# A hybrid attention, state-space and expert block on one core: the last gate unit's split, stand-in products, and the place of the embeddings' projection

## The chip, the cores and the metric

One core of a Trainium2 chip runs the whole kernel in one launch. The metric is the device time of an execution in microseconds, and of several executions the median. Engines have these names: PE is TensorE (matmul), PEld its weight loads, DVE is VectorE, ACT is ScalarE, POOL is GpSimd, and SP is SyncE, whose queue issues nearly all loads.

## The reference, cut to what matters

One layer on 256 tokens of width 1024, all in fp32. A mixer (attention of 8 heads beside a state-space scan) adds to `x`; then a mixture of 16 experts, in which each token uses two; then a gate on token embeddings `p`; then a norm.

```python
h2 = rms_norm(x, ffn_norm_g)
x = x + hier_moe(h2, w_rg, b_rg, w_re, b_re, w_gate, w_up, w_down)  # silu(h@w_gate[e]) * (h@w_up[e]) @ w_down[e]
x = x + sigmoid(x @ w_ple_gate) * (p @ w_ple_proj)
return rms_norm(x, final_norm_g)
```

`p` is 256x256, `w_ple_proj` 256x1024 and `w_ple_gate` 1024x1024. All 16 experts' weights are read, 3 x 2 MB each.

## The kernel before, in words

**Tiles and loads.** On-chip memory is cut into 51 buffers of 128x1024 fp32 (`UNITS`, 512 KB each). Weights and intermediate results share them. One list (`pending`, lines 187 to 277) gives the order of all weight loads; `pump` (line 153) takes the next entries from it whenever buffers come free, and issues them on SP's queue at line 160, in order. A first dry pass (`Ring`) counts how many buffers each step holds, so that no load takes a buffer which a later step needs before that load is used up. A load into a buffer waits on the chip for the last reader of the buffer. `consumed` (line 164) gives a weight's buffer back.

The list holds the input projections, the output projections (`wo`, the last of the mixer), then the embeddings `pin` and the two halves `pj` of their projection (`queue_proj`, line 212), then the experts in six blocks: for each block the gate tiles `g`, the up tiles `u` and the down tiles `d`. The first four blocks hold two experts each, and the last two blocks four each. Behind the sixth block's tiles come the units `pg_0` to `pg_7` of the embeddings' gate, mixed with the last down tiles (`d_r`, the quarters `d_2` and `d_3`) and the final gain.

**Order of the work.** Every engine runs its instructions in the order in which the program emits them; the program below is that order.

1. The mixer, as a list of pieces up to `wo`. Into it hooks are set (`at`, lines 1349 to 1357); the one at `W + 3` runs `pp_T` (line 1306 on), four transposes of `pin` on PE and a copy on ACT.
2. The first chain (lines 1402 to 1420): norm, router logits, `route`, ranks and one-hot matrices. TensorE has gaps here while DVE works. `pp_fill` (line 1324) puts products of the embeddings' projection into them, one 128x256 fp32 product at a time, 16 in all: one at line 1405, five and two in `route` (1000, 1025), two in the first block's gate (1161), and three twice at line 1509. `pp_end` (line 1330) evicts the four results to two buffers, with ACT and DVE.
3. The blocks (loop at line 1475): `gate_up` (matmuls at line 1168), `hidden_T` (1187), `down` (1198) or `half_down` (1455). Before the sixth block stands `overflow`, whose body is under a branch (line 1245) that is not taken unless an expert has too many tokens.
4. The tail (lines 1610 to 1686): the sixth block's down product comes in quarters of 256 columns. Of each quarter, `q_ev` (1445) evicts with ACT (`yh`) and DVE (`yl`), `q_sum` (1527) adds it to the tokens on PE, `q_x2` (1534) adds `x` on DVE, and `q_T` (1540) transposes and splits it. Between them run the gate's products `pg` (lines 389 to 391), for which each unit is split in two parts: `wh_pg` on ACT (line 377) and `wl_pg` on DVE or POOL (line 380). At lines 1641 to 1643 the splits of units 6 and 7 are emitted, and only then the fourth quarter's products and eviction, `q_down(3)`.

Of the kernel before, what the change touches and what calls it, by code (L numbers as in the profile page):

```python
# [92 lines left out]
def emit(ctx, tc, ring, x, p, mix_norm_g, w_in, conv_w, conv_b, dt_bias,  # L93
# [75 lines left out]
    def bank(i, name):  # L169
        return psum.tile([P, 512], F32, tag=f"b{i}", name=name)  # L170
# [44 lines left out]
            pending.append((f"pj_{i}", rows(w_ple_proj, i * P * D, 1, D, D), 1))  # L215

    queue_tok("wo", w_out)
    queue_proj()

    def expert(x, src):  # L220
        if x not in regs:
# [29 lines left out]
    for bl in range(NB):  # L251
        for w, src in (("g", w_gate), ("u", w_up)):
            for c in range(4):
                for e in members(bl):
                    pending.append((f"{w}{e}_{c}", w_rows(e, src, c), 2))
        if bl < NB - 2:
            for c in range(4):
                for e in members(bl):
                    pending.append((f"d{e}_{c}", d_rows(e, c), 1))
        else:  # L260
            queue_half(bl, "h", 0)


# [733 lines left out]

    def route():
        b = MO["lg"]
        pp_fill(5)  # L1000
        for i in range(2):
            dve.scalar_tensor_tensor(rt[:, i, :], b[:, 32 * i:32 * i + 20], rs2[:, i:i + 1], rb, op0=OP.mult,
                                     op1=OP.add)


        v = rt.rearrange("p i (s e) -> p (i s) e", s=5)
        c, df = MO["cmp"]
        for d in (1, 2, 3):
            dve.tensor_tensor(c[:, :, d - 1, 3:7 - d], v[:, :, 0:4 - d], v[:, :, d:4], OP.is_ge)
        above = c if dry else bass.AP(tensor=c.tensor, offset=c.offset + 2, ap=[c.ap[0], [21, 10], [6, 3], [1, 4]])  # L1010
        dve.tensor_tensor(df[:, :, 1:4, :], above, c[:, :, :, 3:7], OP.subtract)
        dve.tensor_reduce(rk, df.rearrange("p s d e -> p s e d"), op=OP.add, axis=AX)
        rv = rk.rearrange("p (i s) e -> p i s e", i=2)
        og, re_ = rc[:, 0:8].rearrange("p (i g) -> p i g", i=2), rv[:, :, 1:5, :]
        be = lambda a: a[:, :, :, None].to_broadcast([P, 2, 4, 4])
        dve.tensor_scalar(og, rv[:, :, 0, :], 0.0, None, op0=OP.is_equal)
        dve.scalar_tensor_tensor(mskb.rearrange("p i (g e) -> p i g e", g=4), re_, 1.5, be(og), op0=OP.is_lt,
                                 op1=OP.mult)
        b = accbank("rank")
        pe.matmul(b[:, 0:16], stri, mskb[:, 0, :], start=True, stop=True)  # L1020
        pe.matmul(b[:, 16:32], stri, mskb[:, 1, :], start=True, stop=False)
        pe.matmul(b[:, 16:32], onesb, mskb[:, 0, :], start=False, stop=True)
        for i in range(2):
            pe.matmul(b[:, 32:48], onesb, mskb[:, i, :], start=(i == 0), stop=(i == 1))
        pp_fill(2)
        MO["count"] = b[:, 32:48]
        MO["rank"] = b[:, 0:32].rearrange("p (i e) -> p i e", i=2)

        def weights():

            gl, el = rt[:, :, 0:4], rt[:, :, 4:20].rearrange("p i (g e) -> p i g e", g=4)
            o1, o2, d = (o12[:, j].rearrange("p i (g e) -> p i g e", g=4) for j in range(3))
            gx = rc[:, 8:16].rearrange("p (i g) -> p i g", i=2)
            gmax, gsum, sv, w1, w2 = (rc[:, 16 + 2 * j:18 + 2 * j] for j in range(5))
            bg = lambda a: a[:, :, None].to_broadcast([P, 2, 4])
            b4 = lambda a: a[:, :, None, None].to_broadcast([P, 2, 4, 4])
            dve.tensor_reduce(gmax, gl, op=OP.max, axis=AX)
            dve.tensor_scalar(o1, re_, 0.0, None, op0=OP.is_equal)
            dve.tensor_scalar(o2, re_, 1.0, None, op0=OP.is_equal)
            dve.tensor_tensor(gx, gl, bg(gmax), OP.subtract)  # L1040
            dve.tensor_tensor(d, o1, o2, OP.subtract)
            act.activation(gx, gx, AF.Exp)
            dve.tensor_tensor(o1, o1, be(og), OP.mult)
            dve.tensor_tensor(d, d, be(og), OP.mult)
            dve.tensor_tensor(o2, o2, be(og), OP.mult)
            dve.tensor_tensor(d, d, el, OP.mult)
            dve.tensor_reduce(sv, o12[:, 2], op=OP.add, axis=AX)
            dve.tensor_reduce(gsum, gx, op=OP.add, axis=AX)
            act.activation(sv, sv, AF.Exp, scale=-1.0)
            dve.scalar_tensor_tensor(w1, sv, 1.0, gsum, op0=OP.add, op1=OP.mult)  # L1050
            dve.reciprocal(w1, w1)
            dve.tensor_tensor(w2, sv, w1, OP.mult)
            cb = comb[:, :, 0:16].rearrange("p i (g e) -> p i g e", g=4)
            dve.tensor_copy(comb[:, :, 16], rs2)
            dve.tensor_tensor(o1, o1, b4(w1), OP.mult)
            dve.tensor_tensor(o2, o2, b4(w2), OP.mult)
            dve.tensor_tensor(cb, o1, o2, OP.add)
        return weights
# [92 lines left out]
    def gate_up(pr, mo, beside=None):  # L1151
# [3 lines left out]
        for w in ("g", "u"):  # L1155
            b = accbank(f"{w}{pr}")
            for c in range(4):
                if pr == 0 and w == "g":
                    if c == 0:
                        gather_first()  # L1160
                        pp_fill(2)
                        xg = XT[0]
                    elif c < 3:
                        gather(0, c + 1, c + 2)
                for k in range(2):
                    kk = 2 * c + k
                    for s, e in enumerate(members(pr)):
                        pe.matmul(b[part(pr, s), :], xg.k(kk)[:, part(pr, s, s0)], ready[f"{w}{e}_{c}"][0][:, k, :],  # L1168
                                  start=(kk == 0), stop=(kk == KD - 1), skip_group_check=True)
                for e in members(pr):  # L1170
                    consumed(f"{w}{e}_{c}")
                if beside is not None:
                    next(beside, None)
# [68 lines left out]
    def overflow():  # L1242
# [54 lines left out]
                            pe.matmul(bx[2 * i + hf], ident, o, start=False, stop=False, skip_group_check=True)  # L1297
        ov.free()


    pp = {}

    def pp_T():
        pn = ready["pin"][0]
        pin = pn[:, 0:512].rearrange("p (i f) -> p i f", i=2)
        pp["T"] = pn[:, 512:1024].rearrange("p (k t) -> p k t", k=2)
        b = bank(4, "pT")
        for k in range(2):
            for i in range(2):
                pe.transpose(b[:, T * k + P * i:T * k + P * i + P], pin[:, i, k * P:(k + 1) * P], ident)  # L1310
        act.activation(pp["T"], b.rearrange("p (k t) -> p k t", k=2), AF.Copy)

    def pp_steps():
        for i, hf in ((1, 0), (0, 1), (1, 1), (0, 0)):
            b = bank(2 * i + hf, f"pp{i}{hf}")
            for q in range(2):
                for k in range(2):
                    c = slice(512 * hf + 256 * q, 512 * hf + 256 * q + 256)
                    pe.matmul(b[:, 256 * q:256 * q + 256], pp["T"][:, k, i * P:(i + 1) * P],
                              ready[f"pj_{k}"][0][:, 0, c], start=(k == 0), stop=(k == 1), skip_group_check=True)  # L1320
                    yield
            pp[i, hf] = b

    def pp_fill(n):
        if "g" not in pp:
            pp["g"] = pp_steps()
        for _ in range(n):
            next(pp["g"], None)

    def pp_end():  # L1330
        pp_fill(17)
        pp["t"] = Act("pp", 2).t
        for i, hf in ((1, 0), (0, 1), (1, 1), (0, 0)):
            o = pp["t"][i][:, 512 * hf:512 * hf + 512]
            if hf == 0:
                act.activation(o, pp[i, hf], AF.Copy)
            else:
                dve.tensor_copy(o, pp[i, hf])
        for k in range(2):
            consumed(f"pj_{k}")  # L1340
        consumed("pin")
# [5 lines left out]
        (early if before else hooks).setdefault(i, []).extend(fs)  # L1347

    W = P_OB
    at(W + 3, pp_T)  # L1350
    at(W + 4, lambda: x1_half(0, 0, 4, act))
    at(W + 5, lambda: x1_half(1, 0, 4, dve))
    at(W + 7, lambda: x1_scale(0), ranks_space, lambda: x1_hi(0, 0, 4), lambda: x1_lo(0, pool, 0, 4))
# [48 lines left out]
    x1_scale_end()  # L1402
    x1_half(1, 6, 8, dve)
    x1_logits_sum()
    pp_fill(1)
    x1_logits(6, 8)
    MO["x1T"].free()
    MO["S"] = Act("S", 1, F32R)
# [66 lines left out]
    for pr in range(NB):  # L1475
# [21 lines left out]
        for i in range(2):  # L1497
# [8 lines left out]
                k2 = 2 * (pr % 2) + i  # L1506
                gather(pr // 2 + 1, k2, k2 + 1)
            if pr == 0:
                pp_fill(3)
            if i == 0:  # L1510
                hidden_T(pr, mo)
        if pr == 0:
            pp_end()
        if pr == NB - 2:
            half_down(pr, mo["hT"], cw, "h", 0)
        else:
            down(pr, mo, cw)
# [88 lines left out]
    def store(i, h, q=sp):  # L1606
        s = slice(512 * h, 512 * h + 512)
        q.dma_start(dram(out, i * P * D + 512 * h, [[D, P], [1, 512]]), sc.t[i][:, s])

    half_down(NB - 1, mo["hT"], cw, "h", 0)  # L1610
    q_sum(0)
    q_sum(1)
    pg_split(0)
    q_x2(0)
    q_x2(1)
    q_T(0)
    q_T(1)
    pg_split(1)
    pg(0, 0)
    pg_split(2)  # L1620
# [18 lines left out]
    pg(4, 0)  # L1639
    pg(5, 0)  # L1640
    pg_split(6, False)
    pg_split(7, False)
    q_down(3)
    pg(4, 1, (0,))
    q_sum(3)
    q_x2(3)
# [69 lines left out]
```

## Time and profile before

| | us |
|---|---|
| median of 3 runs | 496.77 (496.36 to 500.08) |
| time of the profiled execution | 498.48 |
| its span, first to last instruction | 496.8 |
| busy in it: PE / PEld / DVE / ACT / POOL | 464.2 / 318.3 / 209.0 / 183.2 / 125.0 |

The profiled execution is one run and not the median one; 1.7 us of its time lie outside the span. A busy PE is not PE at its peak, since ends of matmuls are modelled. In a timeline, what stands in brackets behind a row is the idle time of the engine before it and what ended it. The clock is the share of 2.4 GHz that TensorE was granted: 1.00 is 2.4 GHz, 0.5 would be 1.2 GHz, and a value between is a mix of the two over a stretch.

### The profile page before, as it was taken

How to read it: one execution, taken by the hardware profiler on the slowest of the kernel's cores; microseconds unless marked ns; L12 is line 12 of the kernel's file. 1: busy time of each engine (PE TensorE's matmuls, PEld its weight loads, DVE VectorE, ACT ScalarE, POOL GpSimd, SP SyncE). 2: the span in 40 equal slices, each digit the busy share in tenths (PEclk: the TensorE clock that was granted, in tenths of full speed). 3: DMA queues.
4: the chain of work that ended last, by engine and by line, in shares of the span. 5: the costliest groups of instructions: out<-in, count | busy, mean ns of one | idle time of the engine just before them, and what ended most of it. 6: DMA issues, size and time to landing. Idle time of an engine off the chain costs nothing.

```text
span 496.8 us, 8088 instructions
## 1 busy us (share of the span) xinstructions
PE 464.2 (93%) x3001; PEld 318.3 (64%) x3001; DVE 209.0 (42%) x411; ACT 183.2 (37%) x333; POOL 125.0 (25%) x83
## 2 busy tenths in 40 slices
PE   6999999999999999999999999999999588889981
PEld 5997898999988999998754344353532121126551
DVE  5422587796569576754545111011110000023345
ACT  4646667644676364443532112020110000122233
POOL 3847634534689631042400000000000000010000
PEclk8899999999999999999999999999999899999997
DMA  8899997621423598859458999999999999999902
GB/s 286 241 338 350 350 348 234 201 86 44 127 87 122 174 390 310 271 186 373 161 194 300 393 412 409 409 408 410 409 407 392 405 408 408 396 396 372 369 34 85
DMA packets 73270, 145.25 MB, mean 292 GB/s; under 512 B 8244, under 2 KB 41352, under 8 KB 73224
## 3 DMA queue, kind: packets, MB, share of 16 engines
q1 hardware_dynamic: 72936, 143.89, 80.5%
q10 hardware_dynamic: 288, 0.79, 0.5%
q8 instruction: 25, 0.41, 0.3%
q14 instruction: 21, 0.17, 0.1%
HBM read 143.61 MB, written 1.05 MB: 291 GB/s over the span
## 4 chain that ended last, share of the span: by engine, by line
PE 54%; DMA 33%; DVE 7%; ACT 2%; issue 1%; SPq 1%; POOL 0%; DVEq 0%; ACTq 0%
DMA u<-in_w_up_dram 10%; DMA g<-in_w_gate_dram 10%; PE ac_gb L411 5%; PE ac_ob L411 5%; PE ac_ga L411 5%; DMA d_h<-in_w_down_dram 4%; DMA d<-in_w_down_dram 4%; PE ac_xs L411 3%; PE g L1168 3%; PE u L1168 3%; PE ac_q L411 3%; PE ac_bc L411 2%; PE ac_z L411 2%; PE ac_k L411 2%; DMA d_r<-in_w_down_dram 2%; PE y L1198 2%
## 5 line engine op out<-in xcount | busy, mean ns | idle before, releaser
L1168 PE MATMUL u<-u,XT 128*64 128x512 f32 (+1 forms) x256 | 55.8, 597 | 3.2 <-DMA u<-in_w_up_dram 3.1
L1168 PE MATMUL g<-g,XT 128*64 128x512 f32 (+1 forms) x256 | 50.2, 623 | 6.0 <-PEq L1245 4.6
L380 POOL TENSOR_TENSOR wl_pg<-pg,wh_pg 128x1024 fp32r<-128x1024 f32 x1 | 2.4, 2370 | 199.5 <-PE x L1531 199.5
L1168 PEld LDWEIGHTS u<-u,XT 128*64 128x64 f32 (+1 forms) x256 | 14.3, 123 | 40.4 <-issue 21.6
L1168 PEld LDWEIGHTS g<-g,XT 128*64 128x64 f32 (+1 forms) x256 | 14.2, 127 | 39.3 <-issue 30.0
L1198 PE MATMUL y<-d,mid 128*64 128x512 f32 x128 | 28.3, 595 | 0.0
L1181 DVE SCALAR_TENSOR_TENSOR mid<-u,cwt,mid 128x512 f32<-128x512 f32 x6 | 4.5, 750 | 50.6 <-issue 49.4
L380 POOL TENSOR_TENSOR wl_xs<-xs,wh_xs 128x1024 fp32r<-128x1024 f32 x8 | 19.1, 2393 | 17.7 <-ACT wh_xs L377 7.6
L1144 ACT ACTIVATE sT<-st 128x256 fp32r<-128x256 f32 x6 | 2.3, 385 | 53.0 <-DVE cwt L1143 50.6
L1205 DVE SCALAR_TENSOR_TENSOR yl<-y,cwt,yh 128x512 fp32r<-128x512 f32 x8 | 6.0, 750 | 34.0 <-ACT yh L1204 33.6
L1140 DVE COPY cwt<-st 128x1 f32<-128x1 f32 x6 | 0.9, 158 | 45.3 <-PE st L1135 45.3
L1198 PEld LDWEIGHTS y<-d,mid 128*64 128x64 f32 x128 | 8.8, 137 | 16.7 <-issue 15.4
L759 POOL TENSOR_TENSOR su<-su,su 128x768 f32<-128x768 f32 x8 | 16.9, 2108 | 7.7 <-ACT su L758 7.1
L1188 ACT ACTIVATE mid<-hT 128x512 f32<-128x512 f32 x5 | 3.0, 598 | 34.4 <-PE hT L1187 34.4
L380 POOL TENSOR_TENSOR wl_wo<-wo,wh_wo 128x1024 fp32r<-128x1024 f32 x3 | 7.8, 2615 | 31.0 <-ACT wh_wo L377 29.6
L1204 ACT ACTIVATE yh<-y,cwt 128x512 fp32r<-128x512 f32 x8 | 5.5, 688 | 22.5 <-PE y L1198 22.5
L380 POOL TENSOR_TENSOR wl_z<-z,wh_z 128x1024 fp32r<-128x1024 f32 x4 | 9.6, 2403 | 16.3 <-ACT wh_z L377 7.1
L389 PE MATMUL pg<-wh_pg,x2h 128*128 128x512 f32 x32 | 13.4, 417 | 0.0
L390 PE MATMUL pg<-wl_pg,x2h 128*128 128x512 f32 x32 | 12.9, 403 | 0.5 <-DVE wl_pg L380 0.4
L1119 ACT ACTIVATE XT<-g,gfd 128x256 f32<-128x256 f32 x12 | 5.0, 471 | 21.0 <-PE g L1111 21.0
L391 PE MATMUL pg<-wh_pg,x2l 128*128 128x512 f32 x32 | 12.8, 399 | 0.0
L1111 PE MATMUL g<-S,h2h 128*128 128x256 f32 x44 | 11.5, 295 | 0.6 <-ACT XT L1119 0.6
(418 smaller groups left out, 1173.8 us busy)
## 6 DMA issues: line engine op xcount, KB each, us to landing
g<-in_w_gate_dram SPq DMA_DIRECT2D x64, 512.0 KB, 10.1
u<-in_w_up_dram SPq DMA_DIRECT2D x64, 512.0 KB, 10.1
d<-in_w_down_dram SPq DMA_DIRECT2D x40, 512.0 KB, 9.7
d_h<-in_w_down_dram SPq DMA_DIRECT2D x16, 512.0 KB, 10.4
xs<-in_w_in_dram SPq DMA_DIRECT2D x8, 512.0 KB, 9.8
z<-in_w_in_dram SPq DMA_DIRECT2D x8, 512.0 KB, 8.7
ga<-in_w_in_dram SPq DMA_DIRECT2D x8, 512.0 KB, 8.7
gb<-in_w_in_dram SPq DMA_DIRECT2D x8, 512.0 KB, 4.8
```

What stands on the lines that cost most here:

```text
L380: (pool if pool_lo else dve).tensor_tensor(l, src, h.bitcast(F32), OP.subtract)
L389: pe.matmul(o, lh, rh, start=start, stop=False, skip_group_check=skip)
L390: pe.matmul(o, lh, rl, start=False, stop=False, skip_group_check=skip)
L391: pe.matmul(o, ll, rh, start=False, stop=stop, skip_group_check=skip)
L411: pe.matmul(st["b"][:, T * f:T * f + T], w[:, k, 128 * f:128 * f + 128], x_.k(kk), start=(n + kk + f == 0), stop=(n == 2 and kk == 4 * k_u ...
L759: pool.tensor_tensor(e, e, cbm[:, t // 4:t // 4 + 1, :].to_broadcast([P, 2, 384]), OP.mult)
L1111: pe.matmul(b[:, 256 * k:256 * k + 256], MO[hs, i].t[0][:, kk * P:(kk + 1) * P], S, start=(first and n == 0 and k == 0), stop=(last and n ...
L1119: act.activation(o[:, 256 * k:256 * k + 256], b[:, 256 * k:256 * k + 256], AF.Copy, scale=g2[:, k:k + 1])
L1168: pe.matmul(b[part(pr, s), :], xg.k(kk)[:, part(pr, s, s0)], ready[f"{w}{e}_{c}"][0][:, k, :], start=(kk == 0), stop=(kk == KD - 1), skip_ ...
L1198: pe.matmul(by[hf][part(pr, s), :], mo["hT"][:, c, part(pr, s)], w[:, 0, 512 * hf:512 * hf + 512], start=(c == 0), stop=(c == 3), skip_gro ...
L1204: act.activation(mo["yh"][:, sl], by[hf], AF.Copy, scale=cw)
L1205: dve.scalar_tensor_tensor(mo["yl"][:, sl], by[hf], cw, mo["yh"][:, sl].bitcast(F32), op0=OP.mult, op1=OP.subtract)
```

## The change

Four edits:

- `queue_proj` moves from the place behind `wo` to the fifth block, behind its `u` tiles and ahead of its `d_h` tiles.
- `pp_T`, `pp_steps`, `pp_fill` and `pp_end` go. One function `pp_all` does the transposes, the products (eight of 128x512) and the evictions (all on DVE) in one bank, ahead of the fifth block's down products.
- Where `pp_fill` stood, `keep_up` puts products of the identity with 256 columns of `x` into a bank that nothing reads: 1, 5, 2, 2, and 2 twice in place of 3 twice. In the tail `keep_on` puts 2, 3 and 2 more such products.
- The split of gate unit 7 moves behind `q_down(3)`.

```diff
     queue_tok("wo", w_out)
-    queue_proj()
...
         else:
+            if bl == NB - 2:
+                queue_proj()
             queue_half(bl, "h", 0)
...
-        pp_fill(5)
+        keep_up(5)
...
+    def keep_up(n):
+        if "warm" not in MO:
+            MO["warm"] = bank(3, "warm2")
+        for _ in range(n):
+            pe.matmul(MO["warm"][:, 0:256], ident, xt[0][:, 0:256], start=True, stop=True, skip_group_check=True)
...
+    def pp_all():
+        pn = ready["pin"][0]
+        pin = pn[:, 0:512].rearrange("p (i f) -> p i f", i=2)
+        pT = pn[:, 512:1024].rearrange("p (k t) -> p k t", k=2)
+        b = bank(5, "pT")
         for k in range(2):
             for i in range(2):
                 pe.transpose(b[:, T * k + P * i:T * k + P * i + P], pin[:, i, k * P:(k + 1) * P], ident)
+        act.activation(pT, b.rearrange("p (k t) -> p k t", k=2), AF.Copy)
+        pp["t"] = Act("pp", 2).t
+        for i in range(2):
+            for hf in range(2):
+                b = bank(5, f"pp{i}{hf}")
                 for k in range(2):
+                    pe.matmul(b, pT[:, k, i * P:(i + 1) * P], ready[f"pj_{k}"][0][:, 0, 512 * hf:512 * hf + 512],
+                              start=(k == 0), stop=(k == 1))
+                dve.tensor_copy(pp["t"][i][:, 512 * hf:512 * hf + 512], b)
...
-    at(W + 3, pp_T)
...
-    pp_fill(1)
+    keep_up(1)
...
             if pr == 0:
-                pp_fill(3)
+                keep_up(2)
             if i == 0:
                 hidden_T(pr, mo)
-        if pr == 0:
-            pp_end()
         if pr == NB - 2:
+            pp_all()
             half_down(pr, mo["hT"], cw, "h", 0)
...
+    spare = accbank("spare")
+    def keep_on(n):
+        for _ in range(n):
+            pe.matmul(spare[:, 0:256], ident, xt[0][:, 768:1024], start=True, stop=True, skip_group_check=True)
     half_down(NB - 1, mo["hT"], cw, "h", 0)
+    keep_on(2)
     q_sum(0)
     q_sum(1)
+    keep_on(3)
     pg_split(0)
...
     q_T(1)
+    keep_on(2)
     pg_split(1)
...
     pg_split(6, False)
+    q_down(3)
     pg_split(7, False)
-    q_down(3)
```

## Rows read from the trace of the kernel before

**Rows 1.** Page, part 2: DMA's busy tenths in 40 slices of 12.4 us.
```profile
DMA  8899997621423598859458999999999999999902
```

**Rows 2.** Windows: stretch, us, busy PE, PEld, DVE, ACT, POOL, clock, DMA share, GB/s.
```profile
266.00:270.00 4.00, 4.00 (x19) 1.54 (x16) 2.71 (x8) 0.00 (x0) 0.00 (x0) 1.00 0.95 366
...
300.00:380.00 80.00, 79.32 (x440) 31.42 (x439) 10.30 (x25) 10.73 (x20) 0.00 (x0) 1.00 1.03 407
```

**Rows 3.** Timeline of SP, 160 to 305 us: start, length, DMA issues.
```profile
170.47 0.46 SPq L160 DMA_DIRECT2D pin<-in_p_dram  x1
170.99 0.93 SPq L160 DMA_DIRECT2D pj<-in_w_ple_proj_dram  x2
...
228.46 24.69 SPq L160 DMA_DIRECT2D u<-in_w_up_dram  x8
```

**Rows 4.** Waits of SP's queue, 216 to 275 us: total, times, longest.
```profile
SPq L160 <- PE g L1168: 14.2, 3, 8.5
```

**Rows 5.** Chain that ended last, the tail: start, us, step.
```profile
453.03 9.45 DMA d<-in_w_down_dram
```

**Rows 6.** Timeline of TensorE, the tail.
```profile
471.88 2.21 PE L1467 MATMUL y<-d,hTb 128*32 128x256 f32 x32
...
476.12 0.39 PE L1531 MATMUL x<-yh,sT 128*128 128x256 f32 x1 [1.13 <-ACT yh L1447]
```

**Rows 7.** Timeline of ACT, the tail.
```profile
473.41 1.06 ACT L377 ACTIVATE wh_pg<-pg 128x1024 fp32r<-128x1024 f32 x1 [4.21 <-DMA pg<-in_w_ple_gate_dram]
474.65 1.06 ACT L377 ACTIVATE wh_pg<-pg 128x1024 fp32r<-128x1024 f32 x1 [0.18 <-DMA pg<-in_w_ple_gate_dram]
475.61 0.46 ACT L1447 ACTIVATE yh<-y,cwt 128x256 fp32r<-128x256 f32 x1
```

**Rows 8.** The same chain, first chain of the routing and first block.
```profile
228.39 0.44 PE pT L1310 x4
...
271.25 1.30 PE pp L1319 x6
```

**Rows 9.** By tile `pin` and `pp`: ns least, median, most; starts.
```profile
L1311 ACT ACTIVATE pin<-pT x1: 580/580/580, 229.8 to 229.8; 128x512 f32<-128x512 f32 x1
...
L1338 DVE COPY pp<-pp x2: 678/678/679, 270.1 to 270.7; 128x512 f32<-128x512 f32 x2
```

**Rows 10.** Timeline of TensorE, fifth and sixth block.
```profile
368.58 6.20 PE L1168 MATMUL u<-u,XT 128*32 128x512 f32 x50
...
381.88 3.48 PE L1455 MATMUL yh<-d_h,mid 128*32 128x512 f32 x18
...
388.37 1.90 PE L1455 MATMUL yh<-d_h,mid 128*32 128x512 f32 x10 [0.30 <-DMA d_h<-in_w_down_dram]
...
394.90 7.21 PE L1168 MATMUL g<-g,XT 128*32 128x512 f32 x36 [4.63 <-PEq L1245]
...
411.51 2.21 PE L1168 MATMUL u<-u,XT 128*32 128x512 f32 x6
...
429.45 1.90 PE L1168 MATMUL u<-u,XT 128*32 128x512 f32 x10 [0.24 <-DMA u<-in_w_up_dram]
```

**Rows 11.** Windows behind the branch and in the tail, columns as in rows 2.
```profile
395.00:400.00 5.00, 5.00 (x32) 1.62 (x32) 0.00 (x0) 0.00 (x0) 0.00 (x0) 0.67 1.03 406
...
400.00:405.00 5.00, 4.37 (x20) 0.76 (x15) 0.00 (x0) 0.00 (x0) 0.00 (x0) 1.00 1.02 405
...
446.00:460.00 14.00, 13.96 (x73) 8.15 (x72) 5.53 (x8) 5.00 (x7) 1.18 (x1) 1.00 1.07 373
```

**Rows 12.** Timeline of TensorE, sixth block's down products to the third quarter.
```profile
442.81 0.39 PE L1531 MATMUL x<-yh,sT 128*128 128x256 f32 x1 [0.62 <-ACT yh L1447]
...
446.72 0.50 PE L389 MATMUL pg<-wh_pg,x2h 128*128 128x512 f32 x1
...
454.07 4.35 PE L1455 MATMUL yr<-d_r,mid 128*32 128x512 f32 x32
...
462.52 1.91 PE L1467 MATMUL y<-d,hTb 128*32 128x256 f32 x26 [0.46 <-DMA d<-in_w_down_dram]
```

More of the change, by code (lines that the diff above doesn't have):

```diff
@@ L1024, in route @@
             pe.matmul(b[:, 32:48], onesb, mskb[:, i, :], start=(i == 0), stop=(i == 1))
-        pp_fill(2)
+        keep_up(2)
         MO["count"] = b[:, 32:48]
@@ L1160, in gate_up @@
                         gather_first()
-                        pp_fill(2)
+                        keep_up(2)
                         xg = XT[0]
@@ L1298, in overflow @@
         ov.free()
+    def keep_up(n):
[3 more added lines that the diff above has]
+            pe.matmul(MO["warm"][:, 0:256], ident, xt[0][:, 0:256], start=True, stop=True, skip_group_check=True)
     pp = {}
-    def pp_T():
+    def pp_all():
         pn = ready["pin"][0]
         pin = pn[:, 0:512].rearrange("p (i f) -> p i f", i=2)
-        pp["T"] = pn[:, 512:1024].rearrange("p (k t) -> p k t", k=2)
-        b = bank(4, "pT")
+        pT = pn[:, 512:1024].rearrange("p (k t) -> p k t", k=2)
+        b = bank(5, "pT")
         for k in range(2):
@@ L1310, in pp_T @@
                 pe.transpose(b[:, T * k + P * i:T * k + P * i + P], pin[:, i, k * P:(k + 1) * P], ident)
[L1311 to L1316, printed above, removed]
-                for k in range(2):
[L1318 to L1338, printed above, removed]
+        act.activation(pT, b.rearrange("p (k t) -> p k t", k=2), AF.Copy)
[3 more added lines that the diff above has]
+                b = bank(5, f"pp{i}{hf}")
+                for k in range(2):
+                    pe.matmul(b, pT[:, k, i * P:(i + 1) * P], ready[f"pj_{k}"][0][:, 0, 512 * hf:512 * hf + 512],
+                              start=(k == 0), stop=(k == 1))
+                dve.tensor_copy(pp["t"][i][:, 512 * hf:512 * hf + 512], b)
         for k in range(2):
@@ L1508, in emit @@
             if pr == 0:
-                pp_fill(3)
+                keep_up(2)
             if i == 0:
                 hidden_T(pr, mo)
-        if pr == 0:
-            pp_end()
         if pr == NB - 2:
+            pp_all()
             half_down(pr, mo["hT"], cw, "h", 0)
```

## The prediction

> **What bounds the kernel now.** I read the slices of the page first, to see which resource is full in which stage. The DMA digits [rows 1] are low and uneven in the first half, 4 and 5 still in the 20th and 21st slice (236 to 261 us), and from the 23rd they stand at 9 until the 38th: the expert weights. The windows sharpen this [rows 2]: a DMA share of 0.95 between 266 and 270 us, then 1.03 at 407 GB/s over the 80 us from 300. So there are two regimes. Up to about 266 us the loads wait for buffers: SP issued the eight `u` tiles of the second block over 24.7 us [rows 3], and in its list of waits it stands 14.2 us for matmuls of line 1168, which free tiles, in three waits [rows 4]. TensorE's own chain sets that pace. After 266 us the loads are back to back, and what matters is how many bytes are left. That holds into the tail: the last tiles of the third quarter (`d_2`) are a 9.45 us step of the chain that ended last [rows 5].
>
> The end is then a short chain. TensorE finishes the fourth quarter's products (line 1467) at 471.88 + 2.21 = 474.09 us [rows 6]. Their eviction `yh` on ACT starts only at 475.61 [rows 7]. ACT was not waiting for TensorE: it runs in order, and ahead of `yh` stand two splits that each wait for a load, `wh_pg` 6 at 473.41 and `wh_pg` 7 at 474.65. TensorE idles 1.13 us for `yh` [rows 6]. Everything to the end hangs on that eviction: sum, addition, transposes, x2 split, the two low parts, the last products, the gate, the store.
>
> **The change, part by part.**
>
> *The split moved behind the eviction.* `wh_pg` 6 stays ahead. It ends at 473.41 + 1.06 = 474.47, after the products' end at 474.09, so `yh` starts at 474.47 instead of 475.61: **1.14 us** on the path. The moved split then runs from about 474.94 to 476.0. Who waits for it is `wl_pg` 7 on DVE, which comes behind the x2 split and would start near 478.5, so the cover is 2.5 us. It issues no DMA; its two buffers are taken later in program order, its load's place is the same. The chain behind shifts whole, since TensorE has only its idle 1.13 us to lose before it.
>
> *Stand-ins in the first chain.* The real products there (lines 1405, 1000, 1025, 1161) become as many 128x256 fp32 products by the identity, 1+5+2+2: 0. They write bank 3, whose last readers are the additions and squares ahead of the same chain. In the first block 3+3 become 2+2. Three cost 1.30 us [rows 8], so two are worth 0.87 us; the two ACT and two DVE evictions of `pp_end` go too. But this lies after 266 us, where loads set the end: 0. What does count is that the four transposes `pT` leave: 0.44 us of TensorE's chain before the loads saturate [rows 8]. I take **0.4**.
>
> *The projection's loads.* They are `pin`, 0.26 MB, and two `pj`, 0.52 MB each: 1.31 MB, issued at 170.5 to 171.9 us [rows 3], while loads waited for buffers anyway. They move behind the fifth block's `u` tiles, into the saturated stretch: 1.31 MB / 407 GB/s = 3.2 us more to carry there. Against it, the three buffers now take three expert tiles from the start, 1.57 MB, since each later load then takes a buffer three releases sooner. At saturation 1.57 - 1.31 = 0.26 MB more lies in the chip: 0.26 / 407 GB/s = **0.6 us** gained. The first end of the bound is that the buffers bring nothing: 3.2 lost. The other is that the extra bytes fill holes in the tail's transfers: 1.57 / 407 GB/s = 3.9 gained. I take 0.6, because the waits of [rows 4] show buffers, not bandwidth, ahead of 266 us. The page "DMA: Bandwidth & Descriptors" of the Trainium skill (Specifications) gives about 358 GB/s as the HBM limit of a core; the trace shows 407, with one core running, so the measurement stands. By 358 the loss bound would be 3.7 us, an estimate, and the forecast within 0.1 of the same.
>
> *The projection's work.* It is not shown at its new size, so it is built from smaller rows. A 128x256 product costs 1.30 / 3 = 0.43 us [rows 8]; doubled, 0.87 for 512 columns, eight of them 6.9. Four transposes add 0.44, the copy of `pT` 0.58 and three of the four DVE evictions 0.68 each [rows 9], exposed because one bank serves all four products; eight hand-overs of about 0.15 make 1.2 (hT's eviction starts about that long after its transposes). Sum 11.2 us in TensorE's queue, ahead of the fifth block's down products at 381.88 [rows 10]; the bounds are 7.3 (all evictions hidden) and 18 (products at half clock). Queued behind: those products, the branch of line 1245 and the sixth block's gate products. Walk it: 381.9 + 11.2 = 393.1. The last tile that the down products wait for came at 388.37 [rows 10]; even 3.2 later it is there. So they run at the speed of the same 32 in the tail, 4.35 us [rows 12]: 397.4. The pause at the branch, 4.63 [rows 10]: 402.0. Then 64 gate records at 6.20 / 50 = 0.124 us [rows 10] are 7.9; add 1.7 for five us at a granted clock of 0.67 after that pause (a mix of 1.2 and 2.4 GHz), as now [rows 11]: 411.6. Before, the up products began at 411.51. They wait for loads until 429.45, and 7.9 us of work in 18 us of arrivals catches up. So **0**, hidden by the load stream with some 9 us to spare; without that cover 11.2.
>
> *Stand-ins in the tail.* Seven products, 3.0 us. The first two fall into the wait of 0.62 us for `yh` [rows 12], and the sums behind them wait for DVE's `yl` anyway. The three behind put the x2 transposes back by 0.3, the last two put the first gate product from 446.72 to about 447.9. There the splits have then run ahead, and the two slow first records go, so TensorE reaches 454.07 about 0.7 late. Its wait of 0.46 us for `d_2` at 462.52 [rows 12] takes most of that, the rest goes into ACT's wait for `wh_pg` 6. I take **0**; bounds 0 and 3.0. Is there something to gain? A granted clock below 1 would have to be there first. The rows show 0.67 right after the 4.63 us pause, 1.00 in the next five us, and 1.00 from 446 to 460 us [rows 11]: in this run nothing to save. By the page "TensorE: Matmul & The Clock Gate" of the Trainium skill (Part 1), an idle TensorE falls to half clock and activity releases it, so the stand-ins would save slow products here; the trace agrees on the fall after the pause, and shows none in the tail.
>
> **Sum.** 1.14 + 0.4 + 0.6 = 2.1 us off. The profiled execution has a span of 496.80 and a time of 498.48, 1.7 above the median of the runs; the saving is taken off the median: 496.77 - 2.1 = **494.7 us**, 0.4% faster.
>
> **Rivals.**
>
> 1. *Only the split counts, or less.* If the stand-ins' 0.7 us eats into the earlier loads and `wh_pg` 6 still sets `yh`, between 0.5 and 1.1 remain: 495.7 to 496.3. For it: TensorE's wait at 462.52 is only 0.46. It is also the case that the move does nothing, if pg 6 itself comes late: 496.8.
> 2. *The moved bytes cost their full price.* If the three buffers do not bring expert tiles forward, the stream ends 3.2 later: 496.77 + 3.2 - 1.1 = 498.9, slower. It decides from the point where fewer than about 1.6 of the three tiles (0.52 MB or 1.3 us each) are ahead at 266 us. Against: each load ahead of 266 waited for a buffer.
> 3. *The projection is not covered.* If TensorE stays at half clock from the pause on, the projection costs 6.9 more, the down products 4.4, gate and up 7.9 each more: the up products end near 446 instead of 431. Some 5 of the 15 come back, since the down products behind now wait for their loads and then would not: 496.8 + 10 - 1.1, about 506. The point is a loss of 9 us against the walk above. DVE evictions split the new products, which speaks for it; the return to 1.00 after 400 us [rows 11] speaks against.
> 4. *The bytes vanish.* If the three tiles come forward and the projection fits into holes: 496.77 - 3.9 - 0.4 - 1.1 = 491.4.
>
> **How the numbers follow.** Forecast 0.55 (own range 493.4 to 496.0: the 1.0 of the loads and transposes missing or doubled, and 0.3 on either side for the spread of the two close runs), rival 1 0.19, rival 2 0.14, rival 3 0.07, rival 4 0.05. The range 492.4 to 498.9 leaves out rival 3, most of rival 4 and the upper half of rival 2. About 1% (5 us) is what a measurement can tell from no change: rival 4 is faster, rival 3 slower with a little of rival 2's tail, the rest is the same: 0.05, 0.87, 0.08.
>
> **What would show it.** Right: `yh` of the fourth quarter starts as `wh_pg` 6 ends, about 2.1 us earlier in the span; the last load lands 1 us earlier; line 1168's last `u` products wait for loads as before; products of the projection sit in one stretch near 381 to 392. Wrong: the last load lands later than 474.6 (rival 2); no load waits among the sixth block's `u` products, or a granted clock under 1 beyond 405 us (rival 3); TensorE without a wait before `d_2` and late by more than 0.7 (rival 1).

## The result and the profile after

The changed kernel takes **494.91 us** (median of 16 runs, 494.19 to 496.44) against 497.04 for the kernel before on the same chips (16 runs, 496.36 to 500.08): a ratio of 0.9947, with an interval of 0.9932 to 0.9963. Ratios here and below are worked out over all executions, so they are not the quotients of the two medians (0.9957 here). The forecast was 494.7 us. The profiled execution took 494.62 us with a span of 492.9, so 1.7 us lie outside the span as before.

Its span is 3.9 us shorter than that of the profiled execution before, and most of this is not the change. Windows of both kernels over the start, before any code that differs (before first, then after; columns as in rows 2):

```profile
12.00:16.00 4.00, 4.00 (x20) 4.00 (x20) 3.81 (x12) 3.75 (x7) 3.10 (x4) 0.50 1.10 347
```
```profile
12.00:16.00 4.00, 4.00 (x34) 4.00 (x34) 3.06 (x9) 3.81 (x7) 3.47 (x4) 0.95 1.10 348
```

In these 4 us TensorE was granted a clock of 0.50 in one execution and 0.95 in the other, and 20 products stand against 34. So times in two spans can't be set side by side. I take an anchor that no edit touches, the first product with the output projection's weights, before and after:

```profile
217.31 0.40 PE L389 MATMUL wo<-wh_wo,mh 128*128 128x512 f32 x1
```
```profile
214.81 0.40 PE L390 MATMUL wo<-wh_wo,mh 128*128 128x512 f32 x1
```

They are 2.50 us apart. Every time "from the anchor" below has its own kernel's anchor taken off. Now the tail, ACT of the changed kernel, to be held against [rows 7]:

```profile
471.12 1.06 ACT L378 ACTIVATE wh_pg<-pg 128x1024 fp32r<-128x1024 f32 x1 [4.52 <-DMA pg<-in_w_ple_gate_dram]
472.09 0.46 ACT L1435 ACTIVATE yh<-y,cwt 128x256 fp32r<-128x256 f32 x1
472.44 1.05 ACT L378 ACTIVATE wh_pg<-pg 128x1024 fp32r<-128x1024 f32 x1
```

The eviction `yh` stands right behind unit 6's split and ahead of unit 7's. From the start of unit 6's split to `yh` it was 475.61 - 473.41 = 2.20 us; it is 0.97 now. TensorE, against [rows 6] and [rows 12]:

```profile
451.97 3.84 PE L1443 MATMUL yr<-d_r,mid 128*32 128x512 f32 x32
459.92 1.91 PE L1455 MATMUL y<-d,hTb 128*32 128x256 f32 x26 [0.47 <-DMA d<-in_w_down_dram]
469.28 2.54 PE L1455 MATMUL y<-d,hTb 128*32 128x256 f32 x32
477.42 0.50 PE L391 MATMUL pg<-wl_pg,x2h 128*128 128x512 f32 x1 [0.40 <-DVE wl_pg L381]
```

The idle 1.13 us for `yh` is gone, and what TensorE waits for in the tail is 0.47 for `d_2`, as before, and 0.40 for unit 7's low part, where it was 0.39 before:

```profile
480.94 0.51 PE L390 MATMUL pg<-wl_pg,x2h 128*128 128x512 f32 x1 [0.39 <-DVE wl_pg L380]
```

But look at the load of unit 6: its split, which waited 4.52 us for it, starts at 471.12 - 214.81 = 256.31 from the anchor, and at 473.41 - 217.31 = 256.10 before. In this pair the end of the load stream has not come forward.

The fifth block, TensorE, against [rows 10]:

```profile
375.76 0.60 PE L1318 MATMUL pT<-ident,pin 128*128 128x128 f32 x4
377.04 1.98 PE L1325 MATMUL pp<-pj,pin 128*128 128x512 f32 x4 [0.69 <-ACT pin L1319]
379.81 1.98 PE L1325 MATMUL pp<-pj,pin 128*128 128x512 f32 x4 [0.79 <-DVE pp L1327]
382.58 1.98 PE L1325 MATMUL pp<-pj,pin 128*128 128x512 f32 x4 [0.79 <-DVE pp L1327]
385.35 1.98 PE L1325 MATMUL pp<-pj,pin 128*128 128x512 f32 x4 [0.78 <-DVE pp L1327]
387.26 3.64 PE L1443 MATMUL yh<-d_h,mid 128*32 128x512 f32 x32
394.51 1.80 PE L1169 MATMUL g<-g,XT 128*32 128x512 f32 x8 [3.61 <-PEq L1246]
...
426.64 1.90 PE L1169 MATMUL u<-u,XT 128*32 128x512 f32 x10 [0.23 <-DMA u<-in_w_up_dram]
```

The projection is one stretch of 387.26 - 375.76 = 11.5 us (11.2 were forecast), the down products run behind it without a wait, and the sixth block's up products wait for loads to the end, at 426.64. The chain that ended last says the same: loads from the fifth block to the end.

```profile
372.33 10.52 DMA d_h<-in_w_down_dram
382.97 10.26 DMA g<-in_w_gate_dram
...
461.79 9.31 DMA pg<-in_w_ple_gate_dram
```

What the loads did at the point where they saturate shows in four windows from the anchor, before first:

```profile
217.30:260.80 43.50, 43.28 (x265) 32.85 (x265) 21.27 (x55) 18.98 (x35) 11.47 (x12) 1.00 0.69 241
260.80:268.80 8.00, 8.00 (x42) 2.85 (x38) 5.42 (x24) 0.96 (x2) 0.00 (x0) 1.00 0.83 290
268.80:276.80 8.00, 8.00 (x40) 4.09 (x38) 1.95 (x3) 1.68 (x3) 0.00 (x0) 1.00 0.99 351
276.80:292.80 16.00, 16.00 (x78) 5.60 (x76) 1.88 (x5) 2.34 (x4) 0.00 (x0) 1.00 1.02 402
```
```profile
214.80:258.30 43.50, 43.25 (x263) 32.44 (x261) 21.29 (x55) 18.50 (x34) 11.45 (x12) 1.00 0.71 245
258.30:266.30 8.00, 8.00 (x41) 2.90 (x39) 5.42 (x24) 0.96 (x2) 0.00 (x0) 1.00 0.74 255
266.30:274.30 8.00, 8.00 (x40) 3.62 (x40) 0.75 (x1) 0.60 (x1) 0.00 (x0) 1.00 0.93 323
274.30:290.30 16.00, 16.00 (x78) 5.44 (x74) 1.88 (x5) 2.33 (x4) 0.00 (x0) 1.00 1.03 412
```

The last column is GB/s. In the first 43.5 us the changed kernel moves 4 GB/s more (0.17 MB). In the next two stretches of 8 us it moves 35 and 28 GB/s less: 0.28 + 0.22 = 0.50 MB, of which the last stretch gives 0.16 back. There the kernel before had three buffers coming free beside those that TensorE's expert products give back, when the projection's last products ran (271 us, [rows 8]); the changed kernel has none, and its SP takes 8.65 us over eight gate tiles:

```profile
262.91 8.65 SPq L160 DMA_DIRECT2D g<-in_w_gate_dram  x8
```

That this is why the lead goes is not shown, and run 6 below speaks against it.

### The profile page after: what moved, and what is told of

The parts are those of the page before. It is cut to its first block, busy times and chain, and to the rows that moved or that the text cites. A ratio compares the mean times of both kernels' runs of the same rounds, so it can differ in the third digit from the quotient of the medians.

```text
span 492.9 us, 8145 instructions
## 1 busy us (share of the span) xinstructions
PE 463.7 (94%) x3027; PEld 320.8 (65%) x3027; DVE 208.7 (42%) x413; ACT 181.9 (37%) x331; POOL 124.6 (25%) x83
## 4 chain that ended last, share of the span: by engine, by line
PE 60%; DMA 28%; DVE 6%; ACT 2%; issue 1%; SPq 1%; POOL 0%; DVEq 0%; ACTq 0%
DMA u<-in_w_up_dram 8%; DMA g<-in_w_gate_dram 8%; PE ac_gb L412 5%; PE ac_ob L412 5%; PE ac_ga L412 5%; PE u L1169 4%; DMA d_h<-in_w_down_dram 4%; PE g L1169 4%; PE y L1199 4%; PE ac_xs L412 3%; PE ac_q L412 2%; PE ac_bc L412 2%; PE ac_z L412 2%; PE ac_k L412 2%; DMA d_r<-in_w_down_dram 2%; PE g L1112 2%
## 5 line engine op out<-in xcount | busy, mean ns | idle before, releaser
L1169 PE MATMUL u<-u,XT 128*64 128x512 f32 (+1 forms) x256 | 54.0, 597 | 2.9 <-DMA u<-in_w_up_dram 2.8
L1169 PE MATMUL g<-g,XT 128*64 128x512 f32 (+1 forms) x256 | 48.2, 624 | 4.5 <-PEq L1246 3.6
L391 PE MATMUL pg<-wl_pg,x2h 128*128 128x512 f32 x32 | 12.8, 399 | 0.4 <-DVE wl_pg L381 0.4
L1112 PE MATMUL g<-S,h2h 128*128 128x256 f32 x44 | 11.5, 295 | 0.6 <-ACT XT L1120 0.6
```

What stands on the lines that cost most here:

```text
L391: pe.matmul(o, lh, rl, start=False, stop=False, skip_group_check=skip)
L1112: pe.matmul(b[:, 256 * k:256 * k + 256], MO[hs, i].t[0][:, kk * P:(kk + 1) * P], S, start=(first and n == 0 and k == 0), stop=(last and n ...
```

## Experiments

Each run's median stands beside that of the kernel before in the same batch on the same chip: 498.58 us (35 runs) for the first four, 497.51 (31) for the next four, 497.63 (31) for the last four. All times from the anchor are collected in one table behind them.

**1. The split alone**, on the kernel before.

```diff
-    pg_split(7, False)
     q_down(3)
+    pg_split(7, False)
```

> Only the split of gate unit 7 moves behind the fourth quarter's products; all else is the kernel before. My theory (the parts add, and this one is the eviction's wait): the fourth quarter's yh starts as wh_pg 6 ends, 1.1 us earlier than the kernel before, measured from an instruction ahead of the change; time 1.1 us below before (ratio 0.9977). Rival (the gain comes from the tail stand-ins' clock or from the moved loads): yh moves in the trace but the time moves by less than 0.5 us.

497.83 us, ratio 0.9972 (0.9943 to 1.0001): the interval just takes in no change, so it is the trace that shows the effect. ACT's rows are those of the changed kernel, `yh` behind the first split:

```profile
475.01 1.06 ACT L377 ACTIVATE wh_pg<-pg 128x1024 fp32r<-128x1024 f32 x1 [4.33 <-DMA pg<-in_w_ple_gate_dram]
475.97 0.46 ACT L1447 ACTIVATE yh<-y,cwt 128x256 fp32r<-128x256 f32 x1
476.33 1.04 ACT L377 ACTIVATE wh_pg<-pg 128x1024 fp32r<-128x1024 f32 x1
```

From split to `yh` 0.96 us instead of 2.20. In this execution the load of unit 6 came 0.95 later from the anchor than before, by the same loads in the same order: the stream's end varies between executions, and only differences inside the tail are sharp to 0.1 us.

**2. The tail's stand-ins alone**, on the kernel before (`keep_on` as in the change).

```diff
+    keep_on(2)
     q_sum(0)
     q_sum(1)
+    keep_on(3)
     pg_split(0)
...
     q_T(1)
+    keep_on(2)
     pg_split(1)
```

> Only the seven stand-in products of the tail are added to the kernel before. My theory: 0.7 us later at the d_r products, taken in by the wait for d_2; time within 0.3 us of before. Rival (they carry the part of the gain that the profiled pair does not show, by keeping TensorE at 2.4 GHz in executions where it falls in the tail): 0.7 to 1.0 us below before (ratio 0.998), and fewer long executions.

497.95 us, ratio 0.9999 (0.9970 to 1.0027). Counted from the products with the last `d_h` tile, TensorE comes to the `d_r` products after 452.12 - 437.60 = 14.52 us. In the kernel before it was 454.07 - 440.29 = 13.78 ([rows 12] has the start of its `d_r` products), so 0.74 less. The last `d_h` tile in this run, then before:

```profile
437.60 1.90 PE L1455 MATMUL yh<-d_h,hTb 128*32 128x512 f32 x10 [0.31 <-DMA d_h<-in_w_down_dram]
```
```profile
440.29 1.90 PE L1455 MATMUL yh<-d_h,hTb 128*32 128x512 f32 x10 [0.30 <-DMA d_h<-in_w_down_dram]
```

At the third quarter, where TensorE waits for `d_2` in both, it is level within 0.1 us. In the trace they cost nothing and bring nothing; by the medians an effect of 1 us either way is not excluded.

**3. The projection alone**: the changed kernel with the split back ahead of `q_down(3)` and without `keep_on`.

> The projection in the fifth block, its loads behind that block's u tiles, and stand-ins in the first chain; the split and the tail as before. My theory after the profiled pair: TensorE's chain 0.5 us earlier by the transposes, 0.8 more by two fewer stand-ins, the stream's end only about 0.3 us earlier, time 0.3 us below before. The forecast had 1.0 us below. Rival (the moved 1.31 MB cost their price): 2 to 3 us above.

497.68 us, ratio 0.9990 (0.9962 to 1.0018): undecided. In the profiled execution TensorE waits 1.27 us for `yh`, and then the clock falls:

```profile
477.38 0.39 PE L1518 MATMUL x<-yh,sT 128*128 128x256 f32 x1 [1.27 <-ACT yh L1435]
...
478.92 0.63 PE L391 MATMUL pg<-wl_pg,x2h 128*128 128x512 f32 x1
```
```profile
470.00:475.00 5.00, 4.94 (x43) 3.06 (x42) 1.34 (x2) 0.77 (x2) 0.00 (x0) 1.00 0.73 268
475.00:480.00 5.00, 3.59 (x13) 2.38 (x13) 2.16 (x4) 2.04 (x3) 0.00 (x0) 0.82 0.01 2
480.00:484.00 4.00, 3.60 (x14) 2.53 (x13) 2.10 (x3) 0.60 (x1) 0.00 (x0) 0.80 0.00 0
484.00:488.00 4.00, 4.00 (x19) 3.32 (x18) 2.68 (x4) 2.33 (x5) 0.00 (x0) 1.00 0.00 0
```

A gate product takes 0.63 us instead of 0.40, and from `yh` to the last gate product it is 11.61 us where all others but run 12 have 10.43 to 10.48: a second price of that wait, 1.15 us, in this execution. The kernel before has the same wait and kept its clock in the profiled one.

**4. The change without the tail's stand-ins.**

```diff
-    keep_on(2)
-    keep_on(3)
-    keep_on(2)
```

> The changed kernel without the seven stand-in products in the tail. My theory: the same time as the changed kernel within 0.3 us, 494.6 to 495.2 if before is at 497.0; the first gate product 1.1 us earlier, the d_2 products at the same time. Rival (tail stand-ins carry 0.7 to 1.0): 495.6 to 496.0.

496.95 us, ratio 0.9972 (0.9947 to 0.9997). Clock 1.00 from 438 to 460 us without them, and every tail time within 0.2 us of the changed kernel: in the traces the stand-ins in the tail are not what made it faster. The medians alone don't settle it: the rival that they carry 0.7 to 1.0 us in some executions would give a ratio of 0.997 to 0.998 as well. Against it stands run 2, where they alone bring nothing that shows.

**5. The projection's products four times over**, in the fifth block.

```diff
-                for k in range(2):
-                    pe.matmul(b, pT[:, k, ...], ready[f"pj_{k}"]..., start=(k == 0), stop=(k == 1))
+                for k in range(8):
+                    pe.matmul(b, pT[:, k % 2, ...], ready[f"pj_{k % 2}"]..., start=(k % 2 == 0), stop=(k % 2 == 1))
```

> The changed kernel with the eight products of the embeddings' projection done four times over into the same bank (the same result is left). TensorE's stretch there is 11.5 us in the trace of the changed kernel, 6.9 of it products, so this adds about 20.7 us of TensorE's work in that place and nothing else. Theory (the projection is hidden because the sixth block's up products wait for loads until 426.6 us): the cover is what these 64 products wait, 426.6 - 408.6 = 18.0 us less 7.9 us of their own work, about 10, so some 10 to 11 us of the 20.7 come through, and up to 5 of them come back where later down products no longer wait for loads: 6 to 11 us above the changed kernel. Rival (the move was free because TensorE never sets the time in this stretch): under 2 us above. Rival (there is no cover, the new kernel gained elsewhere what the projection costs): the full 20 us above.

495.83 us, ratio 0.9969 (0.9946 to 0.9991): the trace loses nothing (all times within 0.01 us of the changed kernel from the anchor). My own estimate of 6 to 11 us was wrong. TensorE:

```profile
407.12 3.64 PE L1443 MATMUL yh<-d_h,mid 128*32 128x512 f32 x32
414.52 9.65 PE L1169 MATMUL g<-g,XT 128*32 128x512 f32 x64 [3.75 <-PEq L1246]
...
424.91 7.07 PE L1169 MATMUL u<-u,XT 128*32 128x512 f32 x64
...
437.99 1.90 PE L1443 MATMUL yh<-d_h,hTb 128*32 128x512 f32 x10 [0.30 <-DMA d_h<-in_w_down_dram]
```

The down products start 20.1 us later from the anchor than in the changed kernel (407.12 - 214.56 against 387.26 - 214.81). Then gate and up products run without one wait for a load, and at 437.99 TensorE waits for a load of the next down tiles again. So the cover is about 20 us in all, given back in three places: some 4 us in the gate products, 12.8 in the up products (7.07 instead of 426.64 + 1.90 - 408.63 = 19.9), and the rest behind: at the last down tile TensorE is still 0.76 us late (437.99 - 214.56 against 437.48 - 214.81), which is gone by unit 6's split. I had counted the up products alone.

**6. The projection's loads at their old place**, its work in the fifth block.

```diff
     queue_tok("wo", w_out)
+    queue_proj()
...
-            if bl == NB - 2:
-                queue_proj()
```

> The changed kernel with the three loads of the projection back at their old place behind the output projection's weights; the projection's work stays in the fifth block, so the three buffers are held from 170 us until then. It tells what the move of the loads alone is worth. Prediction's step: 0.6 us later than the changed kernel. Theory after the trace (the 0.25 MB that the changed kernel is ahead at 258 us are lost between 266 and 274 us, where it has no three buffers coming free): within 0.5 of the changed kernel, but here the buffers are not given back in the first block either, so three expert tiles of 1.57 MB stay behind for the whole of the stream less the 1.31 MB carried early: 0 to 0.7 us later. Rival (the buffers bring forward up to three whole tiles): up to 3.9 us later. Rival (moved bytes cost their price): 3 us earlier.

495.12 us, ratio 0.9960 (0.9937 to 0.9984). Unit 6's split starts at 256.65 from the anchor, 0.25 later than the mean of the five kernels with the loads moved (256.40; they lie between 256.31 and 256.50). This run has no buffers coming free at 271 us either, since the projection holds them to the fifth block. Yet in the two stretches in which the changed kernel moved 255 and 323 GB/s it moves 287 and 365, as much as the kernel before (290 and 351):

```profile
258.54:266.54 8.00, 8.00 (x41) 2.94 (x39) 5.42 (x24) 0.96 (x2) 0.00 (x0) 1.00 0.82 287
266.54:274.54 8.00, 8.00 (x40) 3.59 (x42) 0.75 (x1) 0.60 (x1) 0.00 (x0) 1.00 0.96 365
```

So the missing buffers alone do not explain the fall; what sets the changed kernel apart there is that its loads are ahead.

**7. Three buffers fewer** in the changed kernel.

```diff
-UNITS = 51
+UNITS = 48
```

> The changed kernel with 48 buffers in place of 51. It tells what three buffers of 0.52 MB are worth, the term that the prediction set against the 3.2 us of the moved bytes. Prediction's step: 1.57 MB less lie in the chip where the loads saturate, 3.9 us later than the changed kernel. Theory after the trace: the stream's lead is lost where TensorE leaves no buffer free between 266 and 274 us, with three buffers fewer that hole is deeper, so 3 to 5 us later. Rival (TensorE's chain, not buffers, sets when the stream begins): 0 to 1 us later.

498.35 us, ratio 1.0013 (0.9993 to 1.0032), so some 3 us above the changed kernel. Unit 6's split starts at 259.03 from the anchor, 2.63 later than that mean. Runs 6 and 7 both have 48 buffers for expert tiles up to the fifth block; they differ in the 1.31 MB, loaded early in one and inside the stream in the other: 259.03 - 256.65 = 2.38 us. (From the fifth block on run 7 has three buffers fewer too; with the loads back to back there I count this as nothing, which no run shows.) So both terms of the forecast's balance are real: about 2.4 us paid for the moved bytes, 2.6 got for the buffers, each from one pair of executions.

The bytes say the same. Sizes of the load packets that had ended by so many us from the anchor, summed from the traces, MB:

| kernel | 0 | 43.5 | 59.5 | 75.5 |
|---|---|---|---|---|
| before | 49.77 | 60.16 | 65.23 | 71.67 |
| after | 50.03 | 60.57 | 65.13 | 71.73 |
| 6 early loads | 49.77 | 60.26 | 65.43 | 71.71 |
| 7 three buffers fewer | 48.45 | 58.95 | 64.17 | 70.57 |

At the anchor the changed kernel is ahead of the one before by 0.26 MB, to the digit the forecast's balance; 59.5 us later it is not. The three buffers are worth 1.58 MB at the anchor and 1.16 at 75.5 us (after against run 7), the bytes loaded early 1.32 and 1.14 (run 6 against run 7). The leads shrink between 43.5 and 75.5 us; why they shrink there is open.

**8. The final gain's load last in the list**, in the changed kernel.

```diff
     queue_pg(4, 5)
-    pending.append(("fng", ...))
     for e in members(NB - 1):
         pending.append((f"d{e}_3", d_cols(e, 3), 4))
     queue_pg(6, 7)
+    pending.append(("fng", ...))
```

> The changed kernel with the load of the final gain (0.52 MB on chip) put at the very end of the list, behind the gate's units 6 and 7, so that the last quarter's down tiles, and units 6 and 7, land one load earlier, about 1.3 us. Theory (what is left of the loads on the path at the end is small: TensorE waits 0.33 us ahead of the fourth quarter's products and 0.40 us for the low part of unit 7): 0.3 to 0.7 us faster than the changed kernel. Rival (the tail is TensorE's own chain now): 0. Rival (the gain is then late for the last products of the output): slower by up to 1 us.

493.90 us, ratio 0.9926 (0.9901 to 0.9952). ACT's tail:

```profile
469.44 1.06 ACT L378 ACTIVATE wh_pg<-pg 128x1024 fp32r<-128x1024 f32 x1 [2.99 <-DMA pg<-in_w_ple_gate_dram]
471.13 0.47 ACT L1435 ACTIVATE yh<-y,cwt 128x256 fp32r<-128x256 f32 x1 [0.63 <-PE y L1455]
```

`yh` now waits for TensorE's products, no longer for a split, and starts 0.8 us earlier from the anchor. No load stands on the end's path behind the `d_2` tiles, for which TensorE still waits 0.16 us:

```profile
459.77 1.91 PE L1455 MATMUL y<-d,hTb 128*32 128x256 f32 x26 [0.16 <-DMA d<-in_w_down_dram]
```

**9. No stand-ins in the first chain and the first block.**

```diff
-        keep_up(5)
...
-        keep_up(2)
...
-                        keep_up(2)
...
-    keep_up(1)
...
-            if pr == 0:
-                keep_up(2)
```

> The changed kernel without any of the stand-in products in the first chain and the first block (the seven in the tail stay). Prediction's step: they replace real products in TensorE's gaps and change nothing by themselves, 0. Theory after the trace: 0 in the chain; in the first block two products of 0.43 us each lay on TensorE's chain between 266 and 280 us, so at most 0.9 us earlier there, and the load stream takes part of it: 0 to 0.5 us faster. Rival (they keep TensorE's granted clock up through the first chain, where it has gaps): the granted clock falls under 1.00 between 236 and 262 us, and the first gate and up products behind (3.6 and 7.0 us) run slower: 1 to 5 us slower.

496.58 us, ratio 0.9972 (0.9950 to 0.9994); the unaltered change gave 495.44 beside it. Windows of this run, then of the changed kernel:

```profile
244.00:256.00 12.00, 9.77 (x50) 5.88 (x51) 6.32 (x27) 1.31 (x3) 0.00 (x0) 0.73 0.55 197
```
```profile
244.00:256.00 12.00, 12.00 (x72) 7.45 (x72) 5.71 (x23) 2.35 (x8) 0.00 (x0) 1.00 0.58 207
```

Without the stand-ins the clock falls to 0.73 between 244 and 256 us, and the last gate product comes 1.35 us later from the anchor (1.21 later than in run 11). I had expected up to 0.5 us less; the rival, the clock, is what came. So these stand-ins do work: with the real products gone, they keep what those products gave by the way (the clock was 1.00 in the kernel before too, in its window from 217.3 to 260.8 us above). The page "TensorE: Matmul & The Clock Gate" of the Trainium skill (Part 1) says that an idle TensorE falls back to half clock; these two rows agree.

**10. The wait filled, not removed**: two stand-ins in TensorE's idle time ahead of the fourth quarter's sum, on the kernel before.

```diff
     pg(4, 1, (0,))
+    fill = bank(4, "fill")
+    for _ in range(2):
+        pe.matmul(fill[:, 0:256], ident, xt[0][:, 768:1024], start=True, stop=True, skip_group_check=True)
     q_sum(3)
```

> The kernel before, with two stand-in products (identity with 256 columns of x, into a bank that nothing reads) put into TensorE's idle 1.13 us ahead of the fourth quarter's sum; the split of unit 7 stays ahead of the eviction, so the wait stays and is only filled. Theory (the wait has a second price: in some executions TensorE's granted clock falls behind it, as to 0.82 and 0.80 between 475 and 484 us in the run with the projection alone, for 1.15 us): clock 1.00 to the end, and a median 0 to 0.5 us under that of the kernel before, with fewer long executions. Rival (the fall has nothing to do with that wait): no difference, and the clock as before.

496.73 us, ratio 0.9994 (0.9970 to 1.0018): undecided. The median is 0.9 lower, the interval holds both cases, and the profiled execution, its wait down to 0.27 us and its clock 1.00, ends 0.2 later than the kernel before from the anchor.

**11. The change again, unaltered.**

> The changed kernel once more, unaltered, as the neighbour of the other three on the same chip. Theory: its median 2 us under the kernel before, as found. By the traces alone (the anchor being the first product with the output projection, which cancels the start): 1.0 to 1.4 us under. Rival (part of the 2.1 us came from the draw of executions): under 1 us.

495.44 us, ratio 0.9966 (0.9945 to 0.9987). Its median is 2.2 under the kernel before, as at first.

**12. The gain last, and unit 7's low part read last.**

```diff
-            three(pgb[i, hf], ..., c == KD - 1, True)
+            three(pgb[i, hf], ..., c == KD - 1, True, c == 7)   # for unit 7: hi*hi, lo*hi, hi*lo
```

> The changed kernel with the final gain's load at the very end of the list, as in the run before, and with the three products of gate unit 7 in another order: the one that reads the unit's low part last, so that TensorE does not stand for it for 0.40 us. Theory: 0.2 us under the run with the gain alone, 1.0 us under the changed kernel. Rival (DVE and ACT set the end behind the last products): as the run with the gain alone, 0.6 to 0.9 us under the changed kernel.

494.35 us, ratio 0.9940 (0.9912 to 0.9968); TensorE's wait of 0.40 us is 0.17, and its last product comes 0.1 us earlier than in run 8. Runs 8 and 12 are one size by their intervals, and by their traces the fastest of all: 0.8 and 0.9 us ahead of the changed kernel. Their intervals alone don't set them apart from it.

From the anchor, us (worked out from the start times of ACT's two rows, of TensorE's last gate product and of the span's end; one execution each):

| kernel | unit 6's split | `yh` | last gate product | end |
|---|---|---|---|---|
| before | 256.10 | 258.30 | 268.76 | 279.45 |
| 1 split alone | 257.05 | 258.01 | 268.47 | 279.18 |
| 2 tail stand-ins alone | 256.72 | 258.92 | 269.35 | 280.06 |
| 10 wait filled | 256.29 | 258.49 | 268.94 | 279.65 |
| 3 projection alone | 256.44 | 258.75 | 270.36 | 280.72 |
| after | 256.31 | 257.28 | 267.73 | 278.10 |
| 11 after again | 256.43 | 257.40 | 267.87 | 278.25 |
| 4 without tail stand-ins | 256.50 | 257.47 | 267.90 | 278.27 |
| 5 projection x4 | 256.31 | 257.27 | 267.73 | 278.10 |
| 6 early loads | 256.65 | 257.61 | 268.04 | 278.40 |
| 7 three buffers fewer | 259.03 | 260.00 | 270.45 | 280.44 |
| 8 gain last | 254.79 | 256.47 | 266.95 | 277.33 |
| 12 gain last, low last | 254.90 | 256.60 | 266.85 | 277.22 |
| 9 no chain stand-ins | 257.65 | 258.62 | 269.08 | 279.45 |

## Why the prediction was right, and where it was not

**The sum by the table.** Unit 6's split: 256.54 on the mean of the four kernels with the old loads, 256.40 of the five with the new ones (3, after, 11, 4, 5): 0.14 off, where the four alone spread over 0.95. From it to `yh`: 2.20 against 0.97, 1.23 off. From `yh` to the last gate product: 10.45 in both (but for runs 3 and 12). From there to the end: 10.70 in the kernels with the projection at its old place, 10.37 in those with the new one, and 9.99 in run 7: 0.33 off. It lies behind the output's last additions and stores, whose rows are the same one by one, so its cause stays open. Together 1.7 us, against 2.1 and 2.2 between the medians.

**The split** was forecast at 1.14 us and gave 1.23, by itself (run 1) as in the whole. `yh` starts as unit 6's split ends, as said; the 0.09 more is that it starts 0.97 us behind the split's start, where the forecast took the split's length of 1.06. The moved split delays nobody: TensorE's wait for unit 7's low part, 0.40 us, was 0.39 before. This is most of the gain.

**The loads** are the step that failed in size. Moved bytes against three buffers were to leave 0.6 us, with 0.4 more for the four transposes; the stream's end moved 0.14 over the kernels, 0.25 in run 6 against them. The sign that was named for it, the last load 1 us earlier, did not come, and whether there is any gain at all is not shown, with 0.95 us between executions. Runs 6 and 7 show why so little is left: the balance is 2.6 - 2.4, where the forecast had 3.9 - 3.2. A buffer more is not a whole tile ahead. The failed step is that the lead at the anchor, 0.26 MB as reckoned, would last: it went where the loads come to saturate, with 0.50 MB less landed in 16 us. The forecast did not allow for that, and why a kernel that is ahead loses its lead there stays open. Rival 2 (498.9, 2.1 us above the kernel before) had the price of the bytes right within a microsecond and fell by the other half of the balance; run 7, which takes the buffers away again, is 0.8 us above its kernel before by the medians, the split's gain and the 0.33 taken in. The transposes did go (TensorE comes to its last product with `wo` 21.46 us from the anchor instead of 21.97), but this lies ahead of a stream whose end did not move by as much.

**The projection's work** was forecast at 11.2 us, hidden with 9 to spare; it took 11.5, and run 5 shows about 20 us of cover for what is added to it. That 11.2 came so near is two misses that cancel: the products took 7.9 us for 6.9, and the four waits between them 3.05 for 3.8. The walk took the sixth block's gate products as running without waits and stopped at the up products; the waits in both and in the down products behind are one reserve, since all of them wait for the same stream. Rival 3 is thereby further off than it was given.

**The stand-ins.** In the tail: 0.7 us late at the `d_r` products and gone at `d_2`'s wait, as forecast, in the traces of runs 2 and 4. In the first chain they were put at 0 because they take the place of real products. That holds for the change as a whole, but it left out what they are for: run 9 shows 1.2 to 1.35 us lost without them.

**What stays open.** That the total came so near (494.91 for 494.7) has some luck in it: the loads with the transposes brought 0.86 us less than forecast, and the medians differ by 0.4 us more than the table's sum. The clock that fell behind the wait for `yh` in run 3 would be such a price in some executions of a kernel with that wait; run 10, made to show it, doesn't decide.

## What to carry to other kernels

On an engine that works in order, look for work that waits for a load ahead of an eviction that is ready: moving one instruction gave 1.2 us here, and moving one 0.5 MB load that is used last behind the ones that are waited for gave 0.8 more. When loads set the pace, price a load moved into the stream together with the buffers that it gives back, and test each alone: they were about 2.4 and 2.6 us, and neither shows in the sum. Before two executions are compared, line them up at an instruction that no edit touches.

## What the runs showed of the hardware

- With the same instructions on TensorE ahead of it, the anchor came between 214.56 us (run 5) and 218.13 (run 3) of the span. In the first 16 us TensorE's granted clock differed between executions: 0.50 from 12 to 16 us in the kernel before and in run 1, 0.95 in the changed kernel, 1.00 in run 5. But run 3, the latest, has 1.00 there too, so this clock does not account for the whole spread.
- An idle time of 1.27 us in the tail was followed by a clock of 0.82 and 0.80 over the next 8 us in run 3, and waits of 1.13 us at the same place in the kernel before and in run 2 by 1.00.
- Counted from the anchor, the start of unit 6's split, which waits for its load, spread over 0.95 us between executions with the same loads in the same order.
